# Gate and up of a SwiGLU layer multiplied in 2 x 2 blocks, three chunk pairs of eight with seven products in place of eight

## The chip, the cores and the metric

One core of a Trainium2 chip runs the whole kernel. The metric is the device time of one execution in microseconds (us); for the kernel before it is 2261.49, the median of three runs (2261.48 to 2262.06).

The engines: TensorE (PE) multiplies matrices, its loads of the stationary operand are shown as PEld; VectorE is DVE, ScalarE is ACT, GpSimd is POOL, and SyncE (SP) issues the loads of the weights. SBUF is the memory that the engines work in, PSUM holds the sums of the matmuls in eight banks.

## The reference

Two layers of a decoder trunk on 256 tokens of width 2048, all in float32. The first half of a layer mixes tokens (attention, a recurrence and a gated linear attention behind one input projection and one output projection); the second half, which the change touches, is the feed-forward part:

```python
h = rms_norm(x, pre_ffn_norm[l])
hid = jax.nn.silu(jnp.einsum('bsd,df->bsf', h, w_ffn_gate[l])) * jnp.einsum('bsd,df->bsf', h, w_ffn_up[l])
ff = jnp.einsum('bsf,fd->bsd', hid, w_ffn_down[l])
x = x + rms_norm(ff, post_ffn_norm[l])
```

`w_ffn_gate` and `w_ffn_up` are 2048 x 5632, `w_ffn_down` is 5632 x 2048.

## The kernel before

**Products.** All large products have the same form. The activations stand transposed in SBUF as `[128, chunks, 256]`: a chunk is 128 of the contracted rows, and its 256 tokens are two halves (t = 0, 1) of 128. Activations and weights are each split into two float32r parts, hi + lo, and a product is three matmuls of 128 x 128 by 128 x 512: hi by hi, hi by lo, lo by hi. So a *unit*, one chunk of weights for one token half, is lines 299, 300 and 301 in `unit`, and a block of 512 output columns is 16 chunks x 2 halves x 3 matmuls = 96, into two PSUM banks (`acc`, of a ring of four).

**Weights.** They pass in the order of use, as pieces of two chunks (`load`, on SyncE's queue, five buffers `raw`), and are split chunk by chunk (`split`): ACT writes the upper part (`act.copy`), DVE the lower (`tensor_tensor` with subtract). The split parts stand in ten buffers (`hilo`, `NHI`), in some blocks also in three of every eight chunks in the tiles `s4` (`wider`). `feed` splits ahead of the product as far as the buffers go, in the FFN up to 12 chunks (`LOOK_W`).

**The order of the program** is made while it is built. `Lane` keeps an estimate of PE's clock; side jobs (norms, transposes, splits of the hidden rows) are cut into the stream of matmuls when their inputs should have come. Every engine works through its own instructions in the order in which they were issued, whatever it has to wait for.

**The FFN.** Its 5632 columns are 11 blocks of 512 in each layer, 22 in all, in three parts of 4, 4 and 3 blocks (`FFN_PARTS`). For each block, `gate` and then `up` are whole blocks of 16 chunks. When a gate half is complete, ACT takes its Silu out of PSUM (`gate`), and when an up half is, DVE multiplies (`up`, a `scalar_tensor_tensor`, tile `sg`). Then the job `hidden` transposes the result on PE (`tpu`) and splits it into `uh` and `ul`. After each part four blocks of `down` follow. The first block of a layer begins while the norm before it is still being worked out (`fresh`); its activations `hh` and `hl` are written chunk by chunk.

Of the kernel before, what the change touches and what calls it, by code (L numbers as in the profile page):

```python
# [10 lines left out]
F32 = mybir.dt.float32  # L11
F32R = mybir.dt.float32r
# [7 lines left out]
P = 128  # L20
# [10 lines left out]
# vec's columns  # L31
# [3 lines left out]
# blocks of w_in: first column and width; the last 16 columns (the low-rank gate) go with the  # L35
# output gate, in two blocks of 264
# [4 lines left out]
FFN_PARTS = ((0, 4), (4, 8), (8, 11))  # L41

NRAW = 5      # raw weights: pieces of 2 chunks
# [7 lines left out]
X_AT = 4      # the piece of weights before which the residual's first part is loaded  # L51
# [3 lines left out]
LOOK_S = 16  # L55
AHEAD = 8
# [58 lines left out]
class Engine:  # L115
    """Issues an engine's instructions and keeps the time at which it will be through with them."""
# [34 lines left out]
def tile_hybrid_trunk(ctx, tc, x, xT, w_in, w_out, w_gate, w_up, w_down, post_norms, lams,  # L151
# [22 lines left out]
    # ---------------------------------------------------------------- constants  # L174
# [12 lines left out]
    # keep[j, i] = 1 where i >= j and both are in one chunk of 64  # L187
# [7 lines left out]
    # 0 at the first position of each chunk of 64, 1 elsewhere  # L195
# [4 lines left out]
    # the exponential's table, ahead of the data  # L200
# [11 lines left out]
    blocks = []  # L212
    for l in range(DEPTH):
        blocks += [(w_in[l][:, n0:n0 + n], range(DC)) for n0, n in IN_ORDER]
        cols = [slice(b * 512, (b + 1) * 512) for b in range(4)]
        blocks += [(w_out[l][:, c], OUT_CHUNKS) for c in cols]
        for f0, f1 in FFN_PARTS:
            for f in range(f0, f1):
                blocks += [(w[l][:, f * 512:(f + 1) * 512], range(DC)) for w in (w_gate, w_up)]
            blocks += [(w_down[l][f0 * 512:f1 * 512, c], range(4 * (f1 - f0))) for c in cols]  # L220
    pieces, starts = [], []
    for src, chunks in blocks:
        starts.append(2 * len(pieces))
        pieces += [(src, chunks[i]) for i in range(0, len(chunks), 2)]
    # the mixer's small tiles take chunks of the other products
    wider = []
    for b, (src, chunks) in enumerate(blocks):
        b %= len(blocks) // DEPTH
        wider += [(b > 13 or (b == 0 and len(wider) > 0)) and i % 8 in (1, 4, 6) for i in range(len(chunks))]
    raws, parts_of, rings = [], [], {False: [], True: []}  # L230
    before_load, before_split = {}, {}

    def load():
        src, c = pieces[len(raws)]
        before = before_load.pop(len(raws), None)
        n = src.shape[1]
        raw = pw.tile([P, 2, 512], F32, tag="raw", name="raw", bufs=NRAW)[:, :, :n]
        for i, k in ((0, 1), (1, 1)) if not raws else ((0, 2),):
            if before is not None:
                before(i, k)  # L240
            there = fetch(raw[:, i:i + k, :], src[(c + i) * P:(c + i + k) * P, :].rearrange("(c p) n -> p c n", p=P))
        raws.append((raw, there))

    def split():
        j = len(parts_of)
        while len(raws) <= j // 2:
            load()
        before_split.pop(j, lambda: None)()
        r, there = raws[j // 2][0][:, j % 2, :], raws[j // 2][1]
        n = r.shape[1]  # L250
# [6 lines left out]
        act.free = max(act.free, there)  # L257
# [4 lines left out]
        if j % 2 and len(raws) < len(pieces):  # L262
            load()

    def feed(upto, used=math.inf):
        """Splits the chunks up to upto, as far as the buffers of used chunks go."""
        while len(parts_of) < min(upto, 2 * len(pieces)):
# [8 lines left out]
    def block(ah, al, nm, evac, skew=0, need=None, fresh=False):  # L276
        """The next block of the stream: [256, n] = activations @ weights; ah, al: [128, chunks,
        256] parts of the activations' transpose. evac(t, sums) takes the sums of half t of the
        tokens. The first half runs ahead of the second by skew chunks, or, where the activations
        are fresh, as they come."""  # L280
        src, chunks = blocks[turn[0]]
        base = starts[turn[0]]
        look = LOOK_W if turn[0] % (len(blocks) // DEPTH) > 13 else LOOK
        turn[0] += 1
        n = src.shape[1]
        acc = [pp.tile([P, 512], F32, tag="acc", name=nm, bufs=4)[:, :n] for _ in range(NT)]
        last = len(chunks) - 1
        at = [0, 0]

        def unit(t):  # L290
            i = at[t]
            c = chunks[i]
# [23 lines left out]
        if not fresh:  # L316
            for step in range(len(chunks) + skew):
# [12 lines left out]
    # ---------------------------------------------------------------- small helpers  # L330
    def rsqrt(y, ss, n, inv, pre=None):
        """y = 1/sqrt(ss * inv (* pre) + eps), elementwise on [128, n]: a guess and 3 Newton steps."""
# [25 lines left out]
    def split_scaled(hi, lo, src, scale):  # L358
        """hi + lo = src * scale (scale: [128, 1] or None), both float32r."""
# [8 lines left out]
    def turned(src, tag, name):  # L368
        """src [128, 512], its four [128, 128] blocks transposed, in PSUM."""
# [19 lines left out]
    def token_scale(sc, wait=True):  # L389
        """sc[:, t] = 1 / rms of the residual's tokens."""  # L390
# [17 lines left out]
    def new_scale():  # L408
        """A tile for the tokens' scales and its columns, to be known before the next evacuation."""
# [56 lines left out]
    def finish(b, mw, ssb, gain, nxt, add=False):  # L466
        """Evacuates block b of a sub-layer's last product: the rows (added to mw's) times the gain,
        and their sums of squares; then the norm."""
        sl = slice(b * 512, (b + 1) * 512)

        def evac(t, acc):
# [11 lines left out]
            if b == 2:  # L483
# [3 lines left out]
                if t == 1:  # L487
                    # the square root's table, ahead of the norm
# [9 lines left out]
    # ---------------------------------------------------------------- start  # L498
# [678 lines left out]
```

## Time and profile before

| | |
|---|---|
| median of the runs | 2261.49 us |
| span of the profiled execution, from its first to its last instruction | 2259.1 us |
| busy: PE, PEld, DVE, ACT | 2242.8, 1837.6, 1341.9, 1158.2 us |
| matmuls of gate and up | 2 x 3 x 704 |
| lower halves of weights on DVE, 512 columns | 1504, mean 687 ns |
| upper halves on ACT, 512 columns | 1504, mean 624 ns |

The time of a run is 2.4 us longer than the span of the profiled execution. In the profile's rows a group is a line, an engine and an operation, with out<-in, the count, the busy time, the mean duration and the idle time before it with what ended it. All instructions that pass through the helper `Engine` have its line 131; they are told apart by their tiles. A row of the timeline is the start, the time up to the last end, and the instructions that it merges (x8); PE's matmuls overlap, so the distance of two starts is shorter than a duration.

### The profile page before, as it was taken

Reading aid. Unit: us, or ns where it says so; the run is one execution under the profiler, and the core shown is the slowest. Engines: PE = TensorE matmul, PEld = TensorE weight load, DVE = VectorE, ACT = ScalarE, POOL = GpSimd, SP = SyncE. Lnnn points to the kernel's source line nnn. Section 1 sums busy time; section 2 is a strip of 40 time slices with the busy share of each in tenths; the row PEclk is TensorE's granted clock in tenths of the full one; section 3 lists DMA queues with packets and bytes.
Section 4 is the critical chain, followed back from the end, with each engine's and each line's share of the span. In section 5 each row is a group of like instructions: output and inputs, shape, how many; then the busy total and the mean of one; then the engine's idle time right before and its main releaser. Section 6 shows DMA issues by size and latency. Waiting matters only on the chain.

```text
span 2259.1 us, 29608 instructions
## 1 busy us (share of the span) xinstructions
PE 2242.8 (99%) x10404; PEld 1837.6 (81%) x10404; DVE 1341.9 (59%) x2521; ACT 1158.2 (51%) x2335; POOL 13.3 (1%) x33
## 2 busy tenths in 40 slices
PE   9999999999999999999999999999999999999998
PEld 7777878888888888888877778788888888888886
DVE  7766866745554555545686667667455454555555
ACT  6555755745444444444464457556444454444443
POOL 0000000000000000000000000000000000000000
PEclk9999999999999999999999999999999999999999
DMA  8553646655565645555544536556565555556553
GB/s 295 168 167 91 216 169 205 198 193 196 177 212 172 207 171 207 190 183 196 193 155 151 160 100 216 177 187 223 170 210 183 193 193 180 198 179 211 169 194 126
DMA packets 220116, 416.87 MB, mean 185 GB/s; under 512 B 13344, under 2 KB 24128, under 8 KB 219968
## 3 DMA queue, kind: packets, MB, share of 16 engines
q1 hardware_dynamic: 218112, 409.75, 54.6%
q0 software_dynamic: 1280, 4.20, 0.8%
q8 instruction: 81, 1.33, 0.2%
q10 hardware_dynamic: 576, 1.05, 0.1%
q14 instruction: 67, 0.55, 0.1%
HBM read 412.85 MB, written 2.10 MB: 184 GB/s over the span
## 4 chain that ended last, share of the span: by engine, by line
PE 98%; DVE 1%; ACT 0%; DMA 0%; issue 0%; SPq 0%; DVEq 0%; ACTq 0%
PE in L299 7%; PE gate L301 7%; PE in L301 7%; PE gate L299 7%; PE gate L300 7%; PE up L300 7%; PE up L299 7%; PE up L301 7%; PE in L300 7%; PE down L301 7%; PE down L299 7%; PE down L300 7%; PE op L299 3%; PE op L301 3%; PE op L300 3%; PE sps L675 1%
## 5 line engine op out<-in xcount | busy, mean ns | idle before, releaser
L131 DVE TENSOR_TENSOR hilo<-raw,hilo 128x512 fp32r<-128x512 f32 (+1 forms) x1568 | 999.4, 676 | 583.1 <-ACT hilo L131 582.2
L131 ACT CAST hilo<-raw 128x512 fp32r<-128x512 f32 (+1 forms) x1568 | 900.9, 615 | 524.8 <-DVE hilo L131 307.1
L299 PE MATMUL in<-hilo,hh 128*128 128x512 f32 (+1 forms) x768 | 300.8, 392 | 5.6 <-ACT hilo L131 5.6
L301 PE MATMUL in<-hilo,hl 128*128 128x512 f32 (+1 forms) x768 | 287.6, 374 | 0.8 <-DVE hl L131 0.8
L300 PE MATMUL in<-hilo,hh 128*128 128x512 f32 (+1 forms) x768 | 286.8, 373 | 0.0
L299 PE MATMUL gate<-hilo,hh 128*128 128x512 f32 x704 | 276.1, 392 | 0.0
L299 PE MATMUL down<-hilo,uh 128*128 128x512 f32 x704 | 274.6, 390 | 0.0
L301 PE MATMUL gate<-hilo,hl 128*128 128x512 f32 x704 | 274.4, 390 | 0.1
L301 PE MATMUL down<-hilo,ul 128*128 128x512 f32 x704 | 274.0, 389 | 0.0
L300 PE MATMUL gate<-hilo,hh 128*128 128x512 f32 x704 | 274.0, 389 | 0.0
L300 PE MATMUL down<-hilo,uh 128*128 128x512 f32 x704 | 273.9, 389 | 0.0
L299 PE MATMUL up<-hilo,hh 128*128 128x512 f32 x704 | 273.9, 389 | 0.0
L300 PE MATMUL up<-hilo,hh 128*128 128x512 f32 x704 | 273.9, 389 | 0.0
L301 PE MATMUL up<-hilo,hl 128*128 128x512 f32 x704 | 273.9, 389 | 0.0
L299 PEld LDWEIGHTS in<-hilo,hh 128*128 128x128 f32 x768 | 145.3, 189 | 30.0 <-ACT hilo L131 5.6
L301 PEld LDWEIGHTS in<-hilo,hl 128*128 128x128 f32 x768 | 144.7, 188 | 27.7 <-DVE hl L131 1.3
L300 PEld LDWEIGHTS in<-hilo,hh 128*128 128x128 f32 x768 | 145.3, 189 | 21.5 <-DVE hilo L131 0.8
L301 PEld LDWEIGHTS gate<-hilo,hl 128*128 128x128 f32 x704 | 132.1, 188 | 28.5 <-DVE hl L131 0.9
L301 PEld LDWEIGHTS down<-hilo,ul 128*128 128x128 f32 x704 | 132.2, 188 | 27.5
L299 PEld LDWEIGHTS up<-hilo,hh 128*128 128x128 f32 x704 | 132.2, 188 | 27.4
L301 PEld LDWEIGHTS up<-hilo,hl 128*128 128x128 f32 x704 | 132.2, 188 | 27.4
L300 PEld LDWEIGHTS up<-hilo,hh 128*128 128x128 f32 x704 | 132.2, 188 | 27.4
(187 smaller groups left out, 1989.8 us busy)
## 6 DMA issues: line engine op xcount, KB each, us to landing
raw<-in_w_gate_dram SPq DMA_DIRECT2D x176, 512.0 KB, 4.7
raw<-in_w_up_dram SPq DMA_DIRECT2D x176, 512.0 KB, 4.6
raw<-in_w_down_dram SPq DMA_DIRECT2D x176, 512.0 KB, 5.1
raw<-in_w_in_dram SPq DMA_DIRECT2D x159, 512.0 KB, 4.2
raw<-in_w_out_dram SPq DMA_DIRECT2D x64, 512.0 KB, 4.6
raw<-in_w_in_dram SPq DMA_DIRECT2D x32, 264.0 KB, 2.9
gain<-in_post_norms_dram POOLq DMA_DIRECT2D x16, 256.0 KB, 4.0
x<-in_x_dram SPq DMA_DIRECT2D x8, 256.0 KB, 7.5
```

Source lines behind the costliest of these rows:

```text
L131: return getattr(self.engine, name)(*args, **kwargs)
L299: nc.tensor.matmul(acc[t], ah[:, c, sl], hi, start=(i == 0), stop=False)
L300: nc.tensor.matmul(acc[t], ah[:, c, sl], lo, start=False, stop=False)
L301: nc.tensor.matmul(acc[t], al[:, c, sl], hi, start=False, stop=(i == last))
L675: nc.tensor.matmul(sps[:, m, :nk], qT[r0, h, qt * P:(qt + 1) * P], kT[r0, h, :nk], start=True, stop=False)
```

## The change

Gate and up of a block are multiplied together. Their weights come in one array `w_gu`, which is laid out on the host in the order of use, so a piece of two chunks holds gate or up chunks as `pair_order` names them. Two chunks (c, c + 1), the two token halves and the two matrices make a product of 2 x 2 blocks: a11, a21 are the halves of chunk c, a12, a22 those of chunk c + 1; b11 and b12 are gate and up of chunk c, b21 and b22 of chunk c + 1.

Five of the eight chunk pairs of a block (C) are multiplied as before, eight units. Three (S) take seven units: p1 = a11 b11, p2 = a12 b21, p6 = s2 t2, p7 = s3 t3, q4 = a22 t4, q3 = s4 b22 and q5 = s1 t1. The s are sums of activations, made once a layer (`make_forms`). The t are sums of weights, made in `split` by four additions on DVE; each t and each b that is used is then split like a chunk, so a pair has seven splits in place of four. The pairs stand in the order CCCSCSCS, in a layer's first block CCCCCSSS.

PSUM: the four banks of `acc` now all belong to one block (p2 and q4 take the gate sums of the two halves too, q3 and x the up sums), and p1, q5, p6 and p7 take the other four, shared with the transposes. When a block ends, `evac` combines the sums: m1 is p1 copied by ACT; u2 = m1 + p6, u3 = u2 + p7, c21 = u3 + q4, c11 = m1 + p2, c12 = q3 - u2 + q5, c22 = x - u3 + q5; then Silu and product as before. The combinations take three of the six tiles `s4` and the activations' forms the other three, so the weights of most FFN blocks have the ten `hilo` buffers alone.

```diff
+PAIRS = "CCCSCSCS"
+FIRST_PAIRS = "CCCCCSSS"
...
+QUAD = ("b11", "t2", "t3", "t4", "b21", "b22", "t1")
...
+    def summed(name, a, b, tag):
+        o = sums[name] = pm.tile([P, 512], F32, tag=tag, name=name, bufs={"rp": 3, "e": 2}[tag])
+        dve.tensor_tensor(out=o, in0=a, in1=b, op=ALU.add)
...
     def split():
...
+        if kind == "b11":
+            up1, gate1, up2 = raw_chunk(i), raw_chunk(i + 1), raw_chunk(i + 3)
+            dve.free = max(dve.free, raws[i // 2 + 1][1])
+            summed("t1", gate1, up1, "e")
+            summed("t2", sums["t1"], up2, "rp")
...
         act.copy(hi, r)
+        if kind == "t2":
+            summed("t3", raw_chunk(i), raw_chunk(i + 3), "rp")
+            summed("t4", sums["t2"], raw_chunk(i + 2), "rp")
...
+        def seven(j, p, final):
...
+            for i, k in enumerate(("p1", "p6", "p7", "q4", "p2", "q3", "q5")):
+                feed(j + i + 1, used[0])
+                multiply(acc[k], a[k], j + i, begin(k), final)
+                used[0] = j + i + 1
+                if final:
+                    evac(k, acc)
+                    feed(base + count + (0, 0, 1, 1, 2, 3, 4)[i], used[0])
+                else:
+                    feed(min(used[0] + LOOK_W, base + count), used[0])
+                lane.tick()
...
+        def make_forms(ah, al):
...
+            dve.tensor_tensor(out=full, in0=ah[:, 2 * N_C:, :].bitcast(F32), in1=al[:, 2 * N_C:, :].bitcast(F32),
+                              op=ALU.add)
...
+            dve.tensor_tensor(out=s1, in0=a21, in1=a22, op=ALU.subtract)
+            dve.tensor_tensor(out=s3, in0=a11, in1=a21, op=ALU.subtract)
+            dve.tensor_tensor(out=s2_, in0=s1, in1=a11, op=ALU.subtract)
+            dve.tensor_tensor(out=s4_, in0=a12, in1=s2_, op=ALU.add)
...
+                    if k == "p1":
...
+                        act.copy(got["m1"], acc["p1"])
+                    if k == "p6":
+                        dve.free = max(dve.free, act.free)
+                        add("u2", got["m1"], acc["p6"])
+                    if k == "p7":
+                        add("u3", got["u2"], acc["p7"])
...
+                    if k == "q4":
+                        add("c21", got["u3"], acc["q4"])
+                    if k == "p2":
+                        add("c11", got["m1"], acc["p2"])
+                    if k == "q3":
+                        add("c12", acc["q3"], got["u2"], ALU.subtract)
+                        add("c22", acc["x"], got["u3"], ALU.subtract)
...
+                    if k == "q5":
+                        for t, g, u in ((0, "c11", "c12"), (1, "c21", "c22")):
+                            add(u, got[u], acc["q5"])
+                        for t, g, u in ((0, "c11", "c12"), (1, "c21", "c22")):
+                            dve.scalar_tensor_tensor(out=got[g], in0=got[u], scalar=s2f[t], in1=got[g],
+                                                     op0=ALU.mult, op1=ALU.mult)
...
-                block(hh, hl, "gate", gate, fresh=(f == 0))
-                block(hh, hl, "up", up)
+                pair_block(f, hh, hl, forms, [(l, "hid", f - 1)] if f else [], evac)
```

Three places of the program, as the instructions stand on their engines. First DVE at the end of a block of gate and up, before: `sg` is the block's product, `hilo` are lower halves of weights, `ul` of the hidden rows.

```order
L131 TENSOR_TENSOR hilo_6356<-raw_6268,hilo_6356 128x512
L131 SCALAR_TENSOR_TENSOR sg_6196<-up_6208,scale_3898,sg_6196 128x512
L131 SCALAR_TENSOR_TENSOR sg_6201<-up_6209,scale_3898,sg_6201 128x512
L131 TENSOR_TENSOR hilo_6367<-raw_6268,hilo_6367 128x512
L131 TENSOR_TENSOR hilo_6380<-raw_6288,hilo_6380 128x512
L131 TENSOR_TENSOR ul_6041<-tpu_6386,uh_6040 128x4x128
```

And the same place now; `hilo_7396`, `7407`, `7419` and `7429` are the first four chunks of the next block:

```order
L158 TENSOR_TENSOR u2_u3_7384<-m1_7383,gu_p67_7202 128x512
L158 TENSOR_TENSOR u2_u3_7384<-u2_u3_7384,gu_p67_7202 128x512
L158 TENSOR_TENSOR hilo_7396<-raw_7257,hilo_7396 128x512
L158 TENSOR_TENSOR c11_c21_7385<-u2_u3_7384,gu_q4_7035 128x512
L158 TENSOR_TENSOR c11_c21_7385<-m1_7383,gu_p2_7034 128x512
L158 TENSOR_TENSOR hilo_7407<-raw_7257,hilo_7407 128x512
L158 TENSOR_TENSOR c12_c22_7386<-gu_q3_7036,u2_u3_7384 128x512
L158 TENSOR_TENSOR c12_c22_7386<-gu_x_7037,u2_u3_7384 128x512
L158 TENSOR_TENSOR hilo_7419<-raw_7286,hilo_7419 128x512
L158 TENSOR_TENSOR c12_c22_7386<-c12_c22_7386,gu_q5_7201 128x512 x2
L158 SCALAR_TENSOR_TENSOR c11_c21_7385<-c12_c22_7386,scale_3898,c11_c21_7385 128x512 x2
L158 TENSOR_TENSOR hilo_7429<-raw_7286,hilo_7429 128x512
```

Between two splits of the next block's chunks there now stand two combinations, and four ahead of the fourth chunk. On PE the transposes of a block's result (`tpu`) stood before in the next block's second chunk:

```order
L299 MATMUL gate_8750<-hilo_8643,hh_3676 128x512
L300 MATMUL gate_8750<-hilo_8643,hh_3676 128x512
L301 MATMUL gate_8750<-hilo_8643,hl_3677 128x512
L376 MATMUL tpu_8764<-ident_77,sg_8574 128x128 x4
L376 MATMUL tpu_8771<-ident_77,sg_8579 128x128 x4
L299 MATMUL gate_8751<-hilo_8643,hh_3676 128x512
```

Now they stand in its fourth, behind a matmul that takes the lower half of that chunk:

```order
L397 MATMUL gu_q3_7436<-hilo_7429,hh_3676 128x512
L398 MATMUL gu_q3_7436<-hilo_7429,hh_3676 128x512
L399 MATMUL gu_q3_7436<-hilo_7429,hl_3677 128x512
L551 MATMUL tpu_7498<-ident_77,c11_c21_7385 128x128 x4
L551 MATMUL tpu_7505<-ident_77,c11_c21_7385 128x128 x4
L397 MATMUL gu_x_7437<-hilo_7429,hh_3676 128x512
```

Third, DVE in the first block of layer 0, before: splits, and the four small instructions that begin the tokens' scale (`ss2` to `scale`).

```order
L131 TENSOR_TENSOR hilo_4053<-raw_3961,hilo_4053 128x512
L131 TENSOR_TENSOR hilo_4064<-raw_3961,hilo_4064 128x512
L131 TENSOR_TENSOR hilo_4077<-raw_3969,hilo_4077 128x512
L131 TENSOR_TENSOR hilo_4088<-raw_3969,hilo_4088 128x512
L131 TENSOR_REDUCE ss2_4099<-ssx_3899 128x2
```

Now, from the last two plain chunks on; `mw_3900` holds the activations' sums, `form` their lower parts:

```order
L158 TENSOR_TENSOR hilo_4063<-raw_3963,hilo_4063 128x512
L158 TENSOR_TENSOR hilo_4074<-raw_3963,hilo_4074 128x512
L158 TENSOR_TENSOR mw_3900<-hh_3676,hl_3677 128x1536
L158 TENSOR_TENSOR mw_3900<-mw_3900 128x3x128 x4
L158 TENSOR_TENSOR form_4092<-mw_3900,form_4092 128x4x128
L158 TENSOR_TENSOR form_4095<-mw_3900,form_4095 128x4x128
L158 TENSOR_TENSOR form_4098<-mw_3900,form_4098 128x4x128
L158 TENSOR_REDUCE ss2_4107<-ssx_3899 128x2
```

The activations' sums have come between the last plain chunk and the first seven-product pair.

More of the change, by code (lines that the diff above doesn't have):

```diff
@@ L41, with pair_order, quad @@
 FFN_PARTS = ((0, 4), (4, 8), (8, 11))
+NF = F // 512
+PAIRS = "CCCSCSCS"
+FIRST_PAIRS = "CCCCCSSS"
+N_C = PAIRS.count("C")
+N_S = PAIRS.count("S")
+def pair_order(f):
+    if f == 0:
+        order = [(m, k) for m in range(2) for k in range(2 * N_C)]
+        return order + [e for p in range(N_C, DC // 2) for e in quad(p)]
+    order, at = [], {"C": 0, "S": N_C}
+    for kind in PAIRS:
+        p = at[kind]
+        at[kind] += 1
+        order += quad(p) if kind == "S" else [(m, k) for m in range(2) for k in (2 * p, 2 * p + 1)]
+    return order
+def quad(p):
+    return [(1, 2 * p), (0, 2 * p), (0, 2 * p + 1), (1, 2 * p + 1)]
 NRAW = 5
@@ L207, in vcol, with plain, add_block @@
         return vec[:, j:j + 1]
-    blocks = []
+    blocks, pieces, starts, piece_starts, items = [], [], [], [], []
+    def plain(src, n_chunks):
+        add_block([src[i * P:(i + 2) * P, :].rearrange("(c p) n -> p c n", p=P) for i in range(0, n_chunks, 2)],
+                  [("raw", i) for i in range(n_chunks)])
+    def add_block(srcs, recipes):
+        b = len(blocks)
+        blocks.append((srcs[0].shape[-1], len(recipes)))
+        starts.append(len(items))
+        piece_starts.append(len(pieces))
+        items.extend((b, kind, 2 * len(pieces) + i) for kind, i in recipes)
+        pieces.extend(srcs)
@@ L213, in tile_hybrid_trunk @@
     for l in range(DEPTH):
[L214 removed]
+        for n0, n in IN_ORDER:
+            plain(w_in[l][:, n0:n0 + n], DC)
         cols = [slice(b * 512, (b + 1) * 512) for b in range(4)]
[L216 removed]
+        for c in cols:
+            plain(w_out[l][:, c], DC)
         for f0, f1 in FFN_PARTS:
             for f in range(f0, f1):
[L219 to L220 removed]
@@ L221, in tile_hybrid_trunk @@
[L221 to L224, printed above, removed]
+                recipes = []
+                for kind in FIRST_PAIRS if f == 0 else PAIRS:
+                    i = sum(1 if r[0] == "raw" else 4 if r[0] == "b11" else 0 for r in recipes)
+                    recipes += [("raw", i + j) for j in range(4)] if kind == "C" else [(name, i) for name in QUAD]
+                add_block([w_gu[l, f, i] for i in range(DC)], recipes)
@@ L226, in tile_hybrid_trunk @@
+            for c in cols:
+                plain(w_down[l][f0 * 512:f1 * 512, c], 4 * (f1 - f0))
+    per_layer = len(blocks) // DEPTH
     wider = []
-    for b, (src, chunks) in enumerate(blocks):
-        b %= len(blocks) // DEPTH
-        wider += [(b > 13 or (b == 0 and len(wider) > 0)) and i % 8 in (1, 4, 6) for i in range(len(chunks))]
+    for b, (n, count) in enumerate(blocks):
+        b %= per_layer
+        w = b in (0, 14, 15, 16, per_layer - 2, per_layer - 1) and len(wider) > 0
+        wider += [w and i % 8 in (1, 4, 6) and (b != 16 or i < 2 * N_C) for i in range(count)]
@@ L230, in tile_hybrid_trunk @@
     raws, parts_of, rings = [], [], {False: [], True: []}
     before_load, before_split = {}, {}
+    sums = {}
     def load():
-        src, c = pieces[len(raws)]
+        src = pieces[len(raws)]
         before = before_load.pop(len(raws), None)
-        n = src.shape[1]
+        n = src.shape[-1]
         raw = pw.tile([P, 2, 512], F32, tag="raw", name="raw", bufs=NRAW)[:, :, :n]
@@ L261, in split @@
         parts_of.append((hi, lo, dve.free))
-        if j % 2 and len(raws) < len(pieces):
+        if (kind == "raw" and i % 2 or kind in ("t2", "b22")) and len(raws) < len(pieces):
             load()
     def feed(upto, used=math.inf):
-        while len(parts_of) < min(upto, 2 * len(pieces)):
+        while len(parts_of) < min(upto, len(items)):
             w = wider[len(parts_of)]
@@ L316, in block @@
         if not fresh:
-            for step in range(len(chunks) + skew):
+            for step in range(count + skew):
                 for t in range(NT):
@@ L534, in tile_hybrid_trunk @@
     for l in range(DEPTH):
-        piece = starts[l * len(blocks) // DEPTH] // 2 + (SMALL_AT if l == 0 else -10)
+        piece = piece_starts[l * per_layer] + (SMALL_AT if l == 0 else -10)
         before_load[piece] = lambda i, k, l=l: load_small(l)
@@ L1073, in tile_hybrid_trunk @@
             for f in range(f0, f1):
[L1074 to L1086 removed]
+                got = {}
@@ new lines, in evac, with add @@
+                def evac(k, acc, got=got, f=f, uh=uh, ul=ul):
+                    def add(name, a, b, op=ALU.add):
+                        dve.tensor_tensor(out=got[name], in0=a, in1=b, op=op)
+                    if k == "p1":
+                        scale_known()
+                        got["m1"] = wide("m1", "on")
+                        for names in (("u2", "u3"), ("c11", "c21"), ("c12", "c22")):
+                            pair = pm.tile([P, 2, 512], F32, tag="s4", name="_".join(names), bufs=NS4)
+                            got[names[0]], got[names[1]] = pair[:, 0, :], pair[:, 1, :]
+                        act.copy(got["m1"], acc["p1"])
[4 more added lines that the diff above has]
+                        add("u3", got["u2"], acc["p7"])
+                        lane.free["sc"] = dve.free + W_DROP
+                    if k == "q4":
[5 more added lines that the diff above has]
+                        add("c22", acc["x"], got["u3"], ALU.subtract)
+                        for t, c in ((1, "c21"), (0, "c11")):
+                            act.activation(got[c], got[c], AF.Silu, scale=s2f[t])
+                    if k == "q5":
[4 more added lines that the diff above has]
+                                                     op0=ALU.mult, op1=ALU.mult)
+                        lane.free["tr"] = lane.free["o"] = dve.free + W_DROP
+                        lane.add(0, hidden(f - f0, f, [got["c11"], got["c21"]], uh, ul))
```

146 lines of the change are left out of this document (121 added, 25 removed).

## The prediction

> **What bounds the kernel now.** I read the page's header, busy times and chain first, then the groups of instructions by shape, then two stretches of the timeline: a block of gate and up in the middle of the FFN, and the first such block of a layer.
>
> ```profile
> span 2259.1 us, 29608 instructions
> PE 2242.8 (99%) x10404; PEld 1837.6 (81%) x10404; DVE 1341.9 (59%) x2521; ACT 1158.2 (51%) x2335; POOL 13.3 (1%) x33
> PE 98%; DVE 1%; ACT 0%; DMA 0%; issue 0%; SPq 0%; DVEq 0%; ACTq 0%
> ```
>
> The chain that ended last is PE for 98%: matmuls removed are time removed, as long as PE is still the last. VectorE and ScalarE have 41% and 49% of the span free. The matmul's price is the distance of two starts, not its duration:
>
> ```profile
> 899.71 0.39 PE L300 MATMUL down<-hilo,uh 128*128 128x512 f32 x1
> ...
> 912.40 0.39 PE L299 MATMUL down<-hilo,uh 128*128 128x512 f32 x1
> ```
>
> These are the first and last of 57 rows in a row: 12.69 us over 56 distances, 0.2267 us each. A unit (one chunk, one token half, three matmuls) is 0.68 us. Next the two stages, first the first block of layer 0, then a later one:
>
> ```profile
> 395.40:440.90 45.50, 45.47 (x210) 37.47 (x209) 33.03 (x78) 33.62 (x79) 0.54 (x1) 1.00 0.62 207
> 950.50:995.00 44.50, 44.50 (x202) 36.95 (x201) 23.32 (x37) 20.92 (x38) 0.00 (x0) 1.00 0.58 189
> ```
>
> After the length come PE, PEld, DVE, ACT, POOL, the granted clock (1.00) and DMA. A later block takes 44.4 us: 192 matmuls (43.5) and the transposes (0.9). PE has no gap in it, DVE is busy for 23 of 44 us. In the first block DVE is already busy for 33.
>
> **What the change removes.** Three chunk pairs of each block need seven products in place of eight, three matmuls each: 9 of 192 matmuls per block, 198 in the 22 blocks, 198 x 0.2267 = 44.9 us. The order on PE has 198 rows fewer too. If PE never waited, a block would take 44.4 - 2.04 = 42.4 us.
>
> **What it adds on DVE.** Per block DVE has 41 lower halves of weights in place of 32, 12 sums t1 to t4, 10 combinations in place of 2, and the 2 lower halves of the hidden rows as before: 65 instructions of 512 columns, two of them scalar_tensor_tensor. What one costs when the next stands ready:
>
> ```profile
> 970.40 1.43 DVE L131 SCALAR_TENSOR_TENSOR sg<-up,scale,sg 128x512 f32<-128x512 f32 x2 [4.77 <-PE up L301]
> 971.75 1.28 DVE L131 TENSOR_TENSOR hilo<-raw,hilo 128x512 fp32r<-128x512 f32 x2
> 974.18 1.29 DVE L131 TENSOR_TENSOR ul<-tpu,uh 128x512 fp32r<-128x512 f32 x2 [1.15 <-ACT uh L131]
> 975.39 4.90 DVE L131 TENSOR_TENSOR hilo<-raw,hilo 128x512 fp32r<-128x512 f32 x8
> 61.13 0.75 DVE L131 SCALAR_TENSOR_TENSOR az<-az 128x4 f32<-128x4 f32 x4
> 974.52 3.75 ACT L131 CAST hilo<-raw 128x512 fp32r<-128x512 f32 x7
> L131 DVE TENSOR_TENSOR hilo<-raw,hilo 128x512 fp32r<-128x512 f32 x1504 | 975.5, 687 | 567.3 <-ACT hilo L131 566.5
> L131 DVE TENSOR_TENSOR hilo<-raw,hilo 128x264 fp32r<-128x264 f32 x64 | 23.8, 414 | 15.7 <-ACT hilo L131 15.7
> L131 ACT CAST uh<-tpu 128x512 fp32r<-128x512 f32 x44 | 23.7, 589 | 127.9 <-PE tpu L376 127.9
> L131 DVE SCALAR_TENSOR_TENSOR hl<-tpx,vec,hh 128x128 fp32r<-128x128 f32 x96 | 26.8, 343 | 4.0 <-ACT hh L131 4.0
> L131 DVE SCALAR_TENSOR_TENSOR sg<-up,scale,sg 128x512 f32<-128x512 f32 x44 | 31.5, 751 | 105.0 <-PE up L301 105.0
> ```
>
> Eight in 4.90 us with 0.69 for the last: one every 0.60 us, though each waits on ScalarE. From PSUM it is the same (974.18 to 975.39 is two). A scalar_tensor_tensor is 0.675 (1.35 for two, 970.40 to 971.75). One that needs the one right before it starts 0.04 after that has ended (four in 0.75, 0.16 each): 0.725. So a block costs DVE 63 x 0.60 + 2 x 0.675 and four dependences of 0.125, 39.7 us, beside PE's 42.4. It fits, but no longer loosely, and the question is where in the block PE meets DVE. ACT has 46 instructions at 0.52 (seven casts in 3.75, the last 0.62) to 0.59, some 25 us, and stays out of it.
>
> **Inside a block** ten split buffers let DVE run ahead. A plain chunk costs DVE 0.60 and PE 1.36, a seven-product pair 6.7 and 4.8. Counting from the fourth chunk on, DVE gains through the plain chunks and has finished the last pair's pieces some 2.9 us before their sums are due. Nothing is lost there. Weights come at one piece of two chunks per 2.04 us when pressed,
>
> ```profile
> 428.90 1.14 ACT L131 CAST hilo<-raw 128x512 fp32r<-128x512 f32 x2 [0.90 <-DMA raw<-in_w_gate_dram]
> 430.94 1.14 ACT L131 CAST hilo<-raw 128x512 fp32r<-128x512 f32 x2 [0.91 <-DMA raw<-in_w_gate_dram]
> ```
>
> and the block needs 16 in 42, or 2.65 us each: hidden. If that cover fails, a wait of about 0.9 us as in these rows would fall on ACT once or twice a block.
>
> **The end of a block** is where PE meets DVE. Before, the rest of a block on DVE was two instructions, and twelve chunks stood split ahead. Now DVE's order is u2, u3, chunk 0, c21, c11, chunk 1, c12, c22, chunk 2, two adds, two products, chunk 3 of the next block; chunk 3 can't be split ahead of this chain. The latencies:
>
> ```profile
> 969.98 0.39 PE L301 MATMUL up<-hilo,hl 128*128 128x512 f32 x1
> ...
> 401.59 1.13 DVE L131 SCALAR_TENSOR_TENSOR hl<-tpx,vec,hh 128x128 fp32r<-128x128 f32 x4 [1.42 <-ACT hh L131]
> ...
> 402.00 0.50 PE L301 MATMUL gate<-hilo,hl 128*128 128x512 f32 x1
> 402.33 0.39 PE L299 MATMUL gate<-hilo,hh 128*128 128x512 f32 x1
> ```
>
> DVE starts 0.42 after the start of the last matmul of a sum (969.98 to 970.40). PE starts 0.07 after DVE's end (401.59 + 0.34, the mean of such an hl, to 402.00), and the matmul behind such a wait comes 0.33 later instead of 0.23: 0.10 for a restart. Let time run from the first matmul of the last pair. The sixth matmul (p6) starts at 1.13, so u2 starts at 1.55 (the copy of p1 on ACT, 0.59, is through at 1.5). To chunk 3 it is 0.725 + 10 x 0.60 + 2 x 0.675 = 8.075; with its own 0.69 and 0.07 PE may use chunk 3's lower half at 10.39. Without waits PE is there after 40 matmuls, 9.07. So PE waits 1.32 us (0.08 of it for c11, whose PSUM bank the next block's first sum takes), in every block. It can hardly be less, as 0.60 is the quickest that the trace shows. Restart: 0.10, taken once a block, since the trace has it; 0 at the other end. With 20 blocks (the first of each layer apart) 26.4 us, and 22 restarts, 2.2.
>
> **The first block of each layer** has its three seven-product pairs in a row behind the plain chunks, and ahead of them the sums of the activations (full, s1 to s4, three splits).
>
> ```profile
> 395.58 0.48 PE L299 MATMUL gate<-hilo,hh 128*128 128x512 f32 x1
> ...
> 414.05 0.69 DVE L131 TENSOR_TENSOR hilo<-raw,hilo 128x512 fp32r<-128x512 f32 x1 [0.44 <-ACT hilo L131]
> ...
> 414.97 0.71 ACT L131 ACTIVATE junk<-x 128x512 f32<-128x512 f32 x1
> ...
> 416.92 0.15 DVE L131 TENSOR_REDUCE ss<-ssx 128x2 f32<-128x8 f32 x1
> 417.60 0.69 DVE L131 TENSOR_TENSOR hilo<-raw,hilo 128x512 fp32r<-128x512 f32 x1
> 418.21 0.15 DVE L131 TENSOR_TENSOR rs_q<-scale 128x2 f32<-128x2 f32 x1
> 419.65 0.69 DVE L131 TENSOR_TENSOR hilo<-raw,hilo 128x512 fp32r<-128x512 f32 x1
> 440.88 1.43 DVE L131 SCALAR_TENSOR_TENSOR sg<-up,scale,sg 128x512 f32<-128x512 f32 x2 [4.77 <-PE up L301]
> ```
>
> PE: from 395.58 to 440.46 (0.42 before 440.88) stand 188 distances, 42.6 us, so transposes and waits take 2.3. The 40 plain units end at 395.58 + 27.2 + 2.3 = 425.1, the three pairs at 439.4. DVE: up to 414.05 its order is the old one, and the last plain chunk is split at about 414.5 (one more square, 0.71, stands ahead of it on ACT, which takes most of the idle 0.44). Then full (512 columns 0.687, 264 columns 0.414, so 1536 some 1.8), three small steps in a chain and their rest (2.2), a cast (0.7), three lower halves (1.8): 421.5. The scale's four small ones take 0.68 (416.92 to 417.60), its eight 1.44 (418.21 to 419.65). The first pair's t2 is split at 426.8, where PE wants it at 426; from there on DVE needs 6.7 us a pair and PE 4.8, so DVE sets the pace. The last t1 is split at 443.3, PE is through at 444.5 instead of 439.4: 5.1 us. And u2 comes only then, at 443.9, so that chunk 3 is ready at 452.7, where PE, from 444.5, would want it at 448.8: 3.9. Together 9.1, for two layers 18.2.
>
> **Sum.** -44.9 + 26.4 + 2.2 + 18.2 = +1.9 us. Span 2259.1 and median 2261.49 differ by 2.4, which the change doesn't touch: 2261.5 + 1.9 = 2263.4 us. Two large terms cancel. With pitches 0.01 off either way (286 in the chains, 3 us), restarts of 0 to 0.2 (2.2 less or more) and the first blocks off by 1 us each, the forecast's own range is 2256 to 2272. A measurement of this kernel tells about 0.2%, 4.5 us, from no change.
>
> **Rivals.** *The first blocks are not late.* If the activations' sums slip in earlier, where ACT keeps DVE idle (0.44 before 414.05), each first block pays only the 1.32: -44.9 + 22 x 1.42 = -13.7, 2247.8 us. Against it stands DVE's order, which has them behind the last plain chunk. Chance 0.22.
>
> *PE doesn't wait at all*, the plain gain: 2216.6 us. It would need DVE to be quicker than the trace ever shows. Chance 0.08.
>
> *DVE becomes the bound* (the other side). If instructions that alternate between kinds follow each other by their full 0.687 and not 0.60, a block takes 63 x 0.687 + 2 x 0.751 + 0.3 = 45.1 us on DVE, against 44.4 before: 20 x 0.7 = 14. A first block then loses 2.6 more in the run of pairs, 1.0 in the chain and 0.9 ahead of it, 13.6 in all, less the 2.04 gained: 2 x 11.6 = 23. Together 2298 us. It decides from the point where 65 instructions fill PE's 43.7 us, at (43.7 - 1.85) / 63 = 0.66 us each. Chance 0.12: the eights in 4.90 speak against it. The Trainium skill has it as a rule (VectorE: DVE Perf Modes, section "The DRAIN you can't avoid"): the next operation doesn't start until the pipe has emptied, though the page adds that one which isn't held starts earlier. By that rule the time would be this rival's; the trace, with 0.60 from start to start at a duration of 0.69, disagrees for splits of one kind, and shows no mixed run.
>
> *Weights come late*: a wait of 0.9 in each of 22 blocks that reaches PE in half of them, 10 us: 2273. The row of 428.90 is for it, the mean need of 2.65 us against it. Chance 0.06.
>
> **How the numbers follow.** The forecast has 0.52: within 0.2% 0.33, slower 0.15, faster 0.04. With the rivals: faster 0.04 + 0.22 + 0.08 = 0.34, same 0.33, slower 0.15 + 0.12 + 0.06 = 0.33. The range leaves out the plain gain and DVE as the bound, 0.20 together: from 2244 (the first rival without most restarts) to 2276 (late weights, with 3 us of pitch).
>
> **What would show it.** Right: PE idle in every block of gate and up, ended by DVE's lower half of chunk 3, about 1.3 us each, blocks about 43.8 us apart; DVE busy for 39 to 40 us of each; the first block of a layer some 7 us longer than the next unhindered block, with waits at p6. Wrong: no idle time on PE at block ends (plain gain), DVE without idle time for a whole block (DVE bound), or ACT waiting on DMA with PE behind it.

## The result, and the profile after

The changed kernel takes 2290.61 us (median of four runs, 2290.54 to 2292.86) where the kernel before took 2261.77 beside it: 1.013 times as long, 95% interval 1.0116 to 1.0145. I had forecast 2263.4 with 2244 to 2276, so it is 27 us later than forecast. The header, the busy times and the chain of the changed kernel:

```profile
span 2288.8 us, 30371 instructions
PE 2217.9 (97%) x10206; PEld 1798.1 (79%) x10206; DVE 1729.3 (76%) x3175; ACT 1277.6 (56%) x2561; POOL 13.3 (1%) x33
PE 85%; DVE 10%; issue 3%; ACT 1%; DMA 1%; SPq 0%; DVEq 0%; ACTq 0%
```

The 198 matmuls are gone from the records (10404 less 10206). But the chain that ended last now runs through DVE for 10%, and no longer through PE alone. What PE waited for, as tile and line, then the releaser, the sum, the number and the longest. The profile leaves the numbers out of names: `gu_p` is the sum p1, p2, p6 or p7, `gu_q` is q3, q4 or q5, `u_u` is the tile of u2 and u3, `c_c` a tile of the combinations c.

```profile
PE gu_p L397 <- DVE u_u L158: 22.8, 22, 2.9
PE gu_q L398 <- DVE hilo L158: 15.3, 15, 1.1
PE gu_p L398 <- DVE hilo L158: 9.0, 10, 1.7
PE down L363 <- DVE hilo L158: 6.3, 6, 1.1
```

The last three rows are waits on lower halves of weights: those of the end of a block that I forecast, and those inside the first blocks (10 in the third row). The first row is the largest, and I had not forecast it: 22 waits, one in every block, of a matmul on u2.

Where it sits is shown by the timeline at the end of a later block, first PE, then DVE:

```profile
489.64 0.39 PE L397 MATMUL gu_p<-hilo,hh 128*128 128x512 f32 x1
...
490.77 0.39 PE L399 MATMUL gu_p<-hilo,form 128*128 128x512 f32 x1
492.01 0.50 PE L397 MATMUL gu_p<-hilo,form 128*128 128x512 f32 x1 [0.85 <-DVE u_u L158]
492.35 0.39 PE L398 MATMUL gu_p<-hilo,form 128*128 128x512 f32 x1
...
501.08 0.50 PE L398 MATMUL gu_q<-hilo,hh 128*128 128x512 f32 x1 [1.06 <-DVE hilo L158]
```

```profile
491.27 0.69 DVE L158 TENSOR_TENSOR u_u<-m,gu_p 128x512 f32<-128x512 f32 x1 [2.80 <-PE gu_p L399]
493.01 0.69 DVE L158 TENSOR_TENSOR u_u<-u_u,gu_p 128x512 f32<-128x512 f32 x1 [1.06 <-PE gu_p L399]
493.62 0.69 DVE L158 TENSOR_TENSOR hilo<-raw,hilo 128x512 fp32r<-128x512 f32 x1
494.22 0.68 DVE L158 TENSOR_TENSOR c_c<-u_u,gu_q 128x512 f32<-128x512 f32 x1
494.82 0.68 DVE L158 TENSOR_TENSOR c_c<-m,gu_p 128x512 f32<-128x512 f32 x1
...
499.01 1.41 DVE L158 SCALAR_TENSOR_TENSOR c_c<-c_c,scale,c_c 128x512 f32<-128x512 f32 x2
500.34 1.89 DVE L158 TENSOR_TENSOR hilo<-raw,hilo 128x512 fp32r<-128x512 f32 x3
```

The row at 489.64 is the first matmul of p1 in the block's last pair, the one at 490.77 the last of p6. p7 should begin 0.23 later, at 491.00. It begins at 492.01, just behind the end of u2 (491.27 + 0.69 = 491.96). p7 doesn't need u2. But in `seven` p6 and p7 are the two halves of one PSUM tile, `gu_p67`; u2 reads p6, and the next matmul that writes into that tile waits for the reader, although it writes the other half. The wait pushes PE back by 1.01 (the row's 0.85 counts from the modelled end of the matmul before), the restart by 0.11. It also pushes u3 back: u3 follows u2 by 1.74 us, and I had 0.725. Behind u3 all goes as forecast: 0.60 from start to start, and from u3 to chunk 3 (500.34) it is 7.33 us (forecast 7.35).

The length of a later block is taken from one group of transposes (`tpu`) to the next in the timeline: it was 44.43 us before and is 44.88 now, in every pair of neighbouring blocks in both layers to within 0.03. One such stretch, with the columns of before:

```profile
456.77:501.65 44.88, 42.97 (x193) 35.02 (x192) 39.85 (x66) 25.90 (x46) 0.00 (x0) 1.00 0.57 188
```

DVE is busy for 39.85 (forecast 39.7), and it stood idle for 2.80 ahead of u2 (2.9).

### The profile page after: what moved, and what is told of

Its sections match the earlier page's. It is cut to its first block, busy times and chain, and to the rows that moved or that the text cites. A ratio compares the mean times of both kernels' runs of the same rounds, so it can differ in the third digit from the quotient of the medians.

```text
span 2288.8 us, 30371 instructions
## 1 busy us (share of the span) xinstructions
PE 2217.9 (97%) x10206; PEld 1798.1 (79%) x10206; DVE 1729.3 (76%) x3175; ACT 1277.6 (56%) x2561; POOL 13.3 (1%) x33
## 4 chain that ended last, share of the span: by engine, by line
PE 85%; DVE 10%; issue 3%; ACT 1%; DMA 1%; SPq 0%; DVEq 0%; ACTq 0%
PE down L363 7%; PE in L362 7%; PE down L364 7%; PE down L362 6%; PE in L364 6%; PE in L363 6%; PE gu_q L398 5%; PE gu_q L399 5%; PE gu_q L397 5%; PE gu_p L397 4%; PE gu_p L399 4%; PE gu_p L398 4%; DVE hilo L158 4%; DVE c_c L158 3%; PE op L362 3%
## 5 line engine op out<-in xcount | busy, mean ns | idle before, releaser
L158 DVE TENSOR_TENSOR hilo<-raw,hilo 128x512 fp32r<-128x512 f32 (+1 forms) x1502 | 965.6, 675 | 343.9 <-ACT hilo L158 341.4
L158 ACT CAST hilo<-raw 128x512 fp32r<-128x512 f32 (+1 forms) x1502 | 857.7, 612 | 369.9 <-DVE hilo L158 183.6
L158 ACT CAST hilo<-t 128x512 fp32r<-128x512 f32 x264 | 162.4, 620 | 178.3 <-DVE t L158 141.9
L398 PE MATMUL gu_q<-hilo,hh 128*128 128x512 f32 x506 | 199.2, 394 | 15.4 <-DVE hilo L158 15.3
L397 PE MATMUL gu_q<-hilo,hh 128*128 128x512 f32 x506 | 197.9, 391 | 0.0
L399 PE MATMUL gu_q<-hilo,hl 128*128 128x512 f32 x506 | 197.7, 391 | 0.1
L158 DVE TENSOR_TENSOR hilo<-t,hilo 128x512 fp32r<-128x512 f32 x264 | 170.4, 684 | 4.4 <-ACT hilo L158 4.4
L363 PEld LDWEIGHTS down<-hilo,uh 128*128 128x128 f32 x704 | 132.2, 188 | 35.9 <-DVE hilo L158 8.8
L362 PEld LDWEIGHTS down<-hilo,uh 128*128 128x128 f32 x704 | 132.1, 188 | 27.1
L398 PE MATMUL gu_p<-hilo,hh 128*128 128x512 f32 x352 | 137.7, 391 | 2.3 <-DVE hilo L158 2.3
L397 PE MATMUL gu_p<-hilo,hh 128*128 128x512 f32 x352 | 137.8, 391 | 0.0
L399 PE MATMUL gu_p<-hilo,hl 128*128 128x512 f32 x352 | 137.3, 390 | 0.0
```

What stands on the lines that cost most here:

```text
L158: return getattr(self.engine, name)(*args, **kwargs)
L362: nc.tensor.matmul(acc[t], ah[:, c, sl], hi, start=(i == 0), stop=False)
L363: nc.tensor.matmul(acc[t], ah[:, c, sl], lo, start=False, stop=False)
L397: nc.tensor.matmul(acc, a[0], hi, start=start, stop=False)
L398: nc.tensor.matmul(acc, a[0], lo, start=False, stop=False)
L399: nc.tensor.matmul(acc, a[1], hi, start=False, stop=stop)
```

## The experiments

A theory and two rivals. **A**: the loss is a matter of order and buffers at the end of a block: the wait on u2 (p6 and p7 in one tile) and the wait on chunk 3 (tenth in DVE's queue behind u2) are paid once a block and add up. **B**: DVE's load, 76% of the span now, sets the pace, and the waits are only where this shows. **C**: the first blocks of the layers hold the loss.

Each of the runs was timed beside the kernel before (2261.3 to 2262.1 us), the one with the long waits in a single run.

**One tile each for p6 and p7.**

```diff
-                acc["p1"] = pp.tile([P, 512], F32, tag="tr", name="gu_p1", bufs=1)
-                acc["q5"] = pp.tile([P, 512], F32, tag="o", name="gu_q5", bufs=1)
-                sc = pp.tile([P, 2, 512], F32, tag="sc", name="gu_p67", bufs=1)
-                acc["p6"], acc["p7"] = sc[:, 0, :], sc[:, 1, :]
+                acc["p6"] = pp.tile([P, 512], F32, tag="tr", name="gu_p6", bufs=1)
+                acc["p7"] = pp.tile([P, 512], F32, tag="o", name="gu_p7", bufs=1)
+                sc = pp.tile([P, 2, 512], F32, tag="sc", name="gu_p1q5", bufs=1)
+                acc["p1"], acc["q5"] = sc[:, 0, :], sc[:, 1, :]
```

> The sums p6 and p7 get a PSUM tile each, and p1 and q5 share the tile of two banks instead; no instruction is added or removed. Theory A (the first matmul of p7 in a block's last pair waits until VectorE has read p6 for u2, because both lie in one tile): PE's wait on u2 goes in every block, u3 follows u2 by 0.7 us instead of 1.7, and the wait on chunk 3's lower half stays at about 1.3 us; later blocks go from 44.8 to 43.7 us, 20 x 1.05 = 21 us, and the first blocks of the two layers lose 3 to 5 us each: 2260 to 2264 us. Theory B (VectorE's load sets the pace of the blocks): nothing changes, 2288 to 2292 us.

Measured: 2267.87 us, ratio 1.0025 (1.0015 to 1.0036): 22.7 us less than the changed kernel, without one instruction less. The row of waits on u2 is gone, u3 follows u2 by 0.79, blocks take 43.92 us, and the wait at the end is this:

```profile
490.35 0.69 DVE L158 TENSOR_TENSOR u_u<-m,gu_p 128x512 f32<-128x512 f32 x1 [2.80 <-PE gu_p L399]
491.14 0.69 DVE L158 TENSOR_TENSOR u_u<-u_u,gu_p 128x512 f32<-128x512 f32 x1
...
498.47 1.89 DVE L158 TENSOR_TENSOR hilo<-raw,hilo 128x512 fp32r<-128x512 f32 x3
```

```profile
499.21 0.50 PE L398 MATMUL gu_q<-hilo,hh 128*128 128x512 f32 x1 [1.26 <-DVE hilo L158]
```

This is the block that I had forecast, with its u2 to chunk 3 of 8.12 us (8.075) and blocks 43.92 apart (43.8). B, which expected no change, is wrong. The time is 4 us over A's range.

**The same, with chunk 3 ahead of the last adds and products.** `feed` inside `seven` splits the next block's chunks up to this number at each of the seven steps:

```diff
-                    feed(base + count + (0, 0, 1, 1, 2, 3, 4)[i], used[0])
+                    feed(base + count + (0, 0, 1, 1, 2, 4, 4)[i], used[0])
```

> As the run with p6 and p7 in tiles of their own, and besides chunk 3 of the next block is split ahead of the block's last two adds and two products. Theory A with my price of the block's end (1.3 us a block, because chunk 3 is the tenth instruction behind u2): chunk 3 comes 2 x 0.60 + 1.35 = 2.5 us earlier, PE no longer waits at the end of a block, blocks take 42.5 us: a further 20 x 1.25 = 25 us and 5 to 8 in the first blocks, 2230 to 2238 us. If VectorE's load sets the pace (theory B), the order of its instructions changes nothing: as the other run.

Measured: 2250.67 us (0.9949, 0.9934 to 0.9964). The direction is A's, the size is not: blocks of 43.16. Chunk 3 is in time, but now chunk 4 is late, behind the same two products:

```profile
497.23 4.90 DVE L158 TENSOR_TENSOR hilo<-raw,hilo 128x512 fp32r<-128x512 f32 x8
497.98 0.50 PE L398 MATMUL gu_p<-hilo,hh 128*128 128x512 f32 x1 [0.50 <-DVE hilo L158]
```

The expectation had taken it that no wait is left once chunk 3 is in time, and had not worked out which chunk comes next.

**Chunks 3 and 4 ahead**: with the tiles apart, and in the changed kernel as it is.

```diff
-                    feed(base + count + (0, 0, 1, 1, 2, 3, 4)[i], used[0])
+                    feed(base + count + (0, 0, 1, 1, 2, 5, 5)[i], used[0])
```

> p6 and p7 in tiles of their own, and both chunk 3 and chunk 4 of the next block split ahead of the block's last two adds and two products. With only chunk 3 ahead a block took 43.16 us and PE still waited 0.5 us (0.65 with the restart) on chunk 4's lower half. Theory A: that wait goes too, blocks take 42.5 us, and the time is 2250.7 - 22 x 0.65 = 2236.4 us (2234 to 2240). If the chain of VectorE's instructions merely moves the wait on to the transposes of the products (they come 1.2 us later), it stays at 2248 to 2252 us.

> The changed kernel, with p6 and p7 still in one tile, and chunks 3 and 4 of the next block split ahead of the last adds and products. Theory A says that the two waits of a block's end add up: the wait on u2 stays (22 rows, 0.85 us and some 0.15 of restart each) and the wait on chunk 3 goes. A block takes 42.4 + 1.1 = 43.5 us in place of 44.88: 2290.6 - 20 x 1.35 - 3 = 2260.5 us (2256 to 2264). If the wait on u2 is itself hidden behind the wait on chunk 3 (one wait seen twice), this run would reach that of the kernel with both mended, 2234 to 2240 us.

Measured: 2235.78 us (0.9884, 0.9869 to 0.9899) with the tiles apart, 2265.11 (1.0018, 1.0008 to 1.0027) without, the one in A's range, the other 1 us above it. A block of the first, and one of the second:

```profile
498.94:541.35 42.41, 42.41 (x192) 35.10 (x191) 39.64 (x66) 25.46 (x46) 0.00 (x0) 1.00 0.61 199
```

```profile
501.88:545.43 43.55, 42.70 (x192) 35.10 (x191) 39.63 (x66) 25.16 (x46) 0.00 (x0) 1.00 0.60 194
```

So the four kernels stand in a square: 44.88 us a block as changed, 43.92 with the tiles apart, 43.55 with the chunks ahead, 42.41 with both. The wait on u2 is worth 1.14 where nothing else is late, the wait on chunk 3 1.51; together they cost 2.47 and not 2.65, because the wait at p7 holds PE up by 1.12 us but DVE's chain by only 0.95 (u3 1.74 behind u2 and not 0.79), so that PE then waits some 0.17 less on chunk 3. The 42.41 is 44.43 less nine matmuls (2.04), to 0.02: nothing else in a later block costs PE time, though DVE still has the same 39.6 us of work in it.

**One pair of eight instead of three.**

```diff
-PAIRS = "CCCSCSCS"
-FIRST_PAIRS = "CCCCCSSS"
+PAIRS = "CCCCCCCS"
+FIRST_PAIRS = "CCCCCCCS"
```

> One chunk pair of eight by seven products in place of three, always the last of the block. It removes 66 matmuls (15.0 us) instead of 198 (44.9). Theory A: the loss lies at the block's end and is paid once a block whatever the number of pairs, 2.4 us in each of 22 blocks, 53 us: 2261.5 - 15 + 53 = 2299 us (2294 to 2302), slower than with three pairs although VectorE is busy for 8 us less of each block; the run of three pairs in the first blocks is gone too, which is worth 10 to 15 us in it, so 2285 if their price is larger than I think. Theory B (VectorE's load): with 57 instructions in place of 65 it is no longer full, and what is left is the gain of 15 us: 2246 to 2255 us.

Measured: 2303.13 us (1.0181, 1.0166 to 1.0197). Less of the change is worse, 1 us beyond A's range, and DVE has time to spare. A block:

```profile
495.62:541.87 46.25, 44.36 (x198) 36.15 (x197) 32.34 (x52) 23.20 (x40) 0.00 (x0) 1.00 0.56 182
```

Without waits the block would take 42.41 + 6 x 0.2267 = 43.77; the other 2.48 is the price of three pairs (2.47), now for one. With DVE busy for 32 of 46 us this excludes B: the loss goes with the number of blocks, not with DVE's load.

**More work on DVE.** In the changed kernel, t1 is made twice:

```diff
             summed("t1", gate1, up1, "e")
+            nc.vector.tensor_tensor(out=sums["t1"], in0=gate1, in1=up1, op=ALU.add)
```

> The sum t1 is made twice in each seven-product pair: 3 more VectorE instructions in a block, 1.8 us, and nothing else. Theory A (VectorE has idle time ahead of u2, 2.8 us in a block, and the waits come from the order at the block's end): later blocks stay at 44.8 us, and only the first blocks, where three pairs in a row are paced by VectorE, grow by about 1.8 us each: 2292 to 2298 us. Theory B: every block grows by 1.8 us, 2290.6 + 22 x 1.8 = 2330 us.

Measured: 2295.29 us (1.0145, 1.0128 to 1.0162), 4.7 more than without; later blocks still take 44.87. That is in A's range, and only the first blocks grew, by 2.8 and 2.3 us from their first matmul to their first transposes, part of it by a slower clock behind a wait that is now 2.3 us (last section).

**Plain first blocks.** `FIRST_PAIRS` is eight plain pairs; the first block has its four sums (p2, q4, q3, x) go to Silu and product as before the change, and `make_forms` stays where it is. While it runs, up to eight chunks of the next block may already be split.

```diff
-FIRST_PAIRS = "CCCCCSSS"
+FIRST_PAIRS = "CCCCCCCC"
...
+                    if k == "up":
+                        for t, g, a in ((0, "c11", "q3"), (1, "c21", "x")):
+                            dve.scalar_tensor_tensor(out=got[g], in0=acc[a], scalar=s2f[t], in1=got[g],
+                                                     op0=ALU.mult, op1=ALU.mult)
```

> The changed kernel, with the first gate and up block of each layer in eight plain chunk pairs as before the change (18 matmuls come back, 4.1 us); the activations' sums are still made there. From the first matmul of that block to the first transpose of its products the changed kernel took 59.9 us, before 47.8; the plain block should be back at about 48 plus at most one wait of 1 us, so the run gains 2 x 10 to 12: 2266 to 2271 us. If the first blocks are not where the time goes (their loss is only moved, as VectorE has to make the sums anyway), it gains less than 6 us: 2285 or more.

Measured: 2271.39 us (1.0042, 1.0027 to 1.0057), 19.2 less than the changed kernel, just above the expected range. From its first matmul to the first transposes such a block takes 47.84 us, as before the change (47.83), with the activations' sums hidden in it. So C is a real part, 9.6 us a layer, and not the whole. The 9.6 is what the first block's three pairs cost net of the nine matmuls that they save, the two waits at that block's own end included, since a plain block has neither. The rest of what the change loses is A's: the later blocks still take 44.87 us.

**All three edits together.**

> All three: tiles of their own for p6 and p7, chunks 3 and 4 ahead, plain first blocks. If the three causes are separate and add up, it takes 20 blocks of 42.5 us where the kernel before had 44.43, and two first blocks as before: 2261.9 - 20 x 1.93 + 2 = 2225 us (2222 to 2229), faster than both kernels by 1.6%. If VectorE's 39.9 us of a block's 42.5 leave too little room, a new wait appears inside the blocks, and it ends above 2235 us.

Measured: 2223.32 us (0.9829, 0.9815 to 0.9844), faster than both kernels. Its header and PE's waits:

```profile
span 2221.1 us, 30305 instructions
PE 2203.8 (99%) x10224; PEld 1802.8 (81%) x10224; DVE 1691.5 (76%) x3117; ACT 1261.1 (57%) x2541; POOL 13.3 (1%) x33
```

```profile
PE in L362 <- ACT hilo L158: 5.8, 1, 5.8
PE in L364 <- DVE hl L158: 0.8, 1, 0.8
PE down L364 <- DVE ul L158: 0.7, 2, 0.4
PE tpx L551 <- DVE hl L158: 0.6, 1, 0.6
```

No wait on gate and up is left; the 5.8 us are at the start of the kernel and were there before the change (5.6).

**How far DVE is from the bound.** t1 made twice and three times in that kernel, with the line shown above:

> The kernel with the three edits together, whose blocks have no wait left, and t1 made twice: 3 more VectorE instructions in each of the 20 later blocks, 1.8 us, 41.7 of PE's 42.4. If VectorE's load decides only once it is over PE's, blocks stay at 42.4 and the time at 2223 to 2226 us. If it decides earlier, because its slack of 2.8 us lies in the wrong place (ahead of u2, behind the plain chunks), waits of up to 0.5 us a block appear, 2228 to 2235 us.

> The same with t1 made three times: 6 more instructions a block, 3.6 us, 43.5 us of VectorE beside PE's 42.4. VectorE should now be the bound: blocks of 43.5 us, 20 x 1.1 = 22 us more than the kernel with the three edits, 2245 us (2240 to 2250). If instructions of VectorE overlapped more than the 0.60 us from start to start that the traces show, it would stay under 2232.

Measured: 2223.60 (0.9834, 0.9818 to 0.985) with three more instructions a block, nothing against 2223.32, and 2247.91 (0.9941, 0.9926 to 0.9956) with six more. A block with six more:

```profile
536.80:580.93 44.13, 42.87 (x192) 34.97 (x191) 43.72 (x72) 25.05 (x47) 0.00 (x0) 1.00 0.59 191
```

Here DVE is busy for 43.72 of 44.13 us: DVE as the bound, B's case, looks like this. The block is 0.6 longer than I expected, but only 14 of the 20 are. The six that come right behind a plain first block or behind `down` lose nothing: a stretch over `down` and such a block takes 129.45 us, and 129.43 with t1 made once. 14 x 1.7 us and the expected 20 x 1.1 come to nearly the same, so it is partly luck that the time fell into its range. In the 14, PE waits 1.25 to 1.28 us at the first matmul behind the block, until just behind the end of c21, which reads q4 out of one of the four banks of `acc`. The bound begins between three and six instructions (1.8 and 3.6 us) beyond what the change put there; the idle time of a block with no wait, 42.41 less 39.64, is 2.8 us.

**Longer waits.** u2 is made again, up to five times, in every second block of the changed kernel, so that the wait ahead of p7 grows. What matters is the clock behind the wait.

```diff
-                        add("u2", got["m1"], acc["p6"])
+                        for _ in range(1 + (f // 2 if f % 2 == 0 else 0)):
+                            nc.vector.tensor_tensor(out=got["u2"], in0=got["m1"], in1=acc["p6"], op=ALU.add)
```

> The changed kernel with u2 made once more in block 2 of each layer, twice more in block 4, and so on up to five times more in block 10: each lengthens PE's wait ahead of p7 by 0.60 us, from 0.85 to 1.5, 2.1, 2.7, 3.3 and 3.9 us. In the first blocks of the changed kernel the matmuls behind the wait of 2.87 us came 0.43 us apart for six distances, and not 0.23. Theory C (one such wait is enough to lower TensorE's granted clock): the matmuls behind the waits of 3.3 and 3.9 us, perhaps 2.7, come 0.43 us apart for 1 to 3 us. Theory D (it was the string of six waits, 7 us idle in the 20 us up to there): no wait in the later blocks lowers the clock, not even 3.9 us. The time is 2290.6 + 2 x (1 + 2 + 3 + 4 + 5) x 0.60 = 2308.6 us by D, 2 to 8 us more by C.

Measured: 2321.5 us, 13 above D's number and 5 above the most that C allowed. Each repetition starts 0.72 us behind the one before and not 0.60 (it writes the tile that the one before it wrote); the ten waits came out 22.6 us longer in all and not 18, which is 4.6 of the 13. The greater part is the clock, so C: one such wait is enough. PE in layer 0, block 4, which has two repetitions:

```profile
716.42 0.65 PE L397 MATMUL gu_p<-hilo,form 128*128 128x512 f32 x1 [2.39 <-DVE u_u L1289]
716.87 0.63 PE L398 MATMUL gu_p<-hilo,form 128*128 128x512 f32 x1
...
719.86 0.45 PE L399 MATMUL gu_p<-hilo,hl 128*128 128x512 f32 x1
720.14 0.39 PE L397 MATMUL gu_q<-hilo,form 128*128 128x512 f32 x1
```

From 716.87 to 719.86 stand seven distances of 0.43, then it is 0.23 again. The granted clock (the last column but two) behind the waits of 3.10 us in block 6, of layer 0 and of layer 1:

```profile
809.40:812.40 3.00, 2.83 (x7) 2.29 (x8) 1.20 (x3) 0.00 (x0) 0.00 (x0) 0.50 0.00 0
1963.40:1966.40 3.00, 2.82 (x12) 2.36 (x13) 1.88 (x5) 0.00 (x0) 0.00 (x0) 1.00 0.00 0
```

The two blocks are alike but for the clock behind that wait. They take 48.64 and 47.08 us, so here the half clock costs 1.6 us, after what PE then waits less on chunk 3.

## Why the prediction was wrong, step by step

**The step that failed** is in "the end of a block": "The sixth matmul (p6) starts at 1.13, so u2 starts at 1.55" and "Without waits PE is there after 40 matmuls, 9.07. So PE waits 1.32 us". The first half held (u2 at 491.27, 1.63 after 489.64, for 1.55). The second let PE run from p6 to chunk 3 with no wait in between. It waits once, at p7, on u2 itself. The tile's two banks are one thing to the order of the program: a reader of one half holds up the writer of the other. The program had shown it: `seven` takes both from one tile, `gu_p67`. The prediction gave the wait no term. Its block is 1.06 us longer than forecast (44.88 against 42.4 + 1.42 = 43.82), 21 us in 20 blocks; the tiles apart give 0.96 of it back, and the other 0.10 is the wait on chunk 3 (below). With the tiles apart the forecast's blocks came out, 43.92, and nearly the time, 2267.87 against 2263.4.

**The first blocks** were sized rightly with the tiles apart. From the first matmul to the first transposes it was 47.83 us and 201 matmuls before; with the tiles apart 58.08 and 204. Less three matmuls that is 9.6 longer (forecast 9.1 and a restart). As changed it is 59.89 in the first layer and 60.48 in the second, 11.4 and 12.0 longer: the wait on u2 again, here 2.87 us, and what comes behind it:

```profile
446.26 0.79 PE L397 MATMUL gu_p<-hilo,form 128*128 128x512 f32 x1 [2.87 <-DVE u_u L158]
446.85 0.63 PE L398 MATMUL gu_p<-hilo,form 128*128 128x512 f32 x1
```

```profile
446.20:449.00 2.80, 2.74 (x7) 2.16 (x8) 1.06 (x3) 0.91 (x1) 0.00 (x0) 0.50 0.44 173
```

The granted clock is 0.50 for five distances here and ten in the other layer, some 1.2 and 2.4 us. The two layers together are 5 us over the forecast. So 21 + 5 of the missing 27 us are accounted for; the last one is not assigned (the first matmul of gate comes 1.3 us later than before, ahead of all that the change touches, and this place lay between 396.41 and 398.58 us in the kernels with the change).

**The gain**, 44.9 us for 198 matmuls, was right: 2.02 a block once no wait is left. **DVE's load** was right too (39.85 against 39.7, 0.60 from start to start). **The wait on chunk 3** was right in place and a little low in size: 1.51 a block with its restart, against 1.42. The 0.08 us of it that I put down to c11 does not show: with the tiles apart the next block's first matmul starts without a gap at 493.48, while c11 runs (492.95 to 493.63). I added that it "can hardly be less". That is wrong: it hung on the order, not on DVE's speed, and two numbers in a list took it away.

**The rivals.** *The first blocks are not late*: wrong, six waits in the first of them. *PE doesn't wait at all*: not this kernel, but the one with all three edits; it took no quicker DVE. *DVE becomes the bound*: the sign came out on its side, for another reason. It needed mixed instructions at their full 0.687; the rows from 493.01 to 494.82 alternate sums and splits at 0.60, with durations of 0.68 and 0.69. The Trainium skill's rule (VectorE: DVE Perf Modes, section "The DRAIN you can't avoid"), that the next operation doesn't start until the pipe has emptied, is thus not borne out in a mixed run either; the Trainium skill's own addition there, that one which isn't held starts earlier, is. *Weights come late*: no wait of PE in gate and up was ended by ACT or by a load.

## What to carry to other kernels

Where a chain of reads follows matmuls closely, ask of each PSUM tile who still writes into it: two sums in one tile are ordered by each other's readers, and a wait that looks like one on data can be one on the neighbour. Price a block's end by the order in which an engine is handed its work before its speed: here one pair cost as much as three, DVE had 2.8 us idle just ahead, and two tiles exchanged and two chunks handed over earlier turned 1.3% slower into 1.2% faster. And when a wait is taken away, work out the next one in the same queue: with chunk 3 in time, chunk 4 still cost 0.75 us a block (43.16 against 42.41).

## What the runs showed of the hardware

- **The clock falls after short idle times.** Behind PE waits of 2.38 to 4.55 us the matmuls came 0.43 us apart, at a granted clock of 0.50, for 5 to 13 distances (1.2 to 3 us lost): in seven of eight of the lengthened waits and in all eight waits of 2.87 or 2.88 us in four kernels. Two waits of 2.29 us, in the first blocks of the kernel that makes t1 twice, did it as well. Behind 0.85 to 1.68 us it never happened, and no run has a wait between 1.68 and 2.29. Behind one of the two waits of 3.10 us it didn't (row of 1963.40). The Trainium skill (TensorE: Matmul & The Clock Gate, section "Part 1: The HAM clock gate") has half the clock after an idle window of some 3.4 us, which runs freely. The half clock agrees; waits of 2.29 us are shorter than that and were enough. A window whose phase decides would fit the one exception; no run here shows it.
- **A restart of PE** behind a wait costs some 0.1 us with the clock at 1.00: 0.34 from the first matmul to the second (492.01 to 492.35), not 0.23; behind some waits of 1.25 us and more it was 0.30 or 0.31.
- **DVE** starts independent sums and splits 0.60 us apart, of one kind or alternating, at durations of 0.68 to 0.69, and one that needs or rewrites the result of the one right before it 0.72 to 0.80 behind it (u2 to u3: 0.79).
